# Half of the one-hot times low-gate products on ScalarE, token by token

## The chip, the cores and the metric

One core of a Trainium2 chip runs the whole program in one launch. The metric is the device time of one execution in microseconds (us); three runs of the kernel before are shown, and their median counts.

## The reference, cut to what matters

Two transformer blocks over 512 tokens of width 1024. The first mixes a pooling branch with a forgetting attention, the second mixes two attentions and ends in a PEER layer: eight heads each choose 16 of 16,384 experts for every token, with a gate each, and the experts' rows are summed.

```python
q = (xt @ w_q).reshape(TOKEN_BLOCK, PEER_HEADS, 2, PEER_HALF_DIM)
sc = jnp.einsum('thcd,chnd->thcn', q, sub_keys, preferred_element_type=jnp.float32)
top_s, top_i = lax.top_k(sc, k)
...
g = jax.nn.softmax(best_s, axis=-1)
pre = jnp.einsum('td,thkd->thk', xt, u[idx], preferred_element_type=jnp.float32)
coef = (g * jax.nn.gelu(pre, approximate=False)).astype(v.dtype)
return jnp.einsum('thk,thkd->td', coef, v[idx])
```

An expert's number is 128 I + J, with I and J between 0 and 127. Only how the gates g are spread over the experts is touched here.

## The kernel before, in words

The first 128 tokens gather their experts' rows by indirect DMA. The other 384 tokens (ND) take all 16,384 experts densely: for each of 128 groups of 128 experts, `u_stage` multiplies the group's u rows by the tokens (24 matmuls of 384 columns), a Gelu follows (`u_gelu`, L1445), the result is multiplied by a dense gate matrix and then by the v rows. Every fp32 operand is split in two fp32r halves: ScalarE writes `hi` (L1389), VectorE the rest `lo` (L1390), and three matmuls (L150 to L152) use them.

The dense gates are built first. `by_slot` (L1579 to L1588) transposes I, J and g of 128 tokens, so that the partition is the slot (head and choice) and the column the token. ScalarE casts I and J to fp16 (`I2`, `J2`) and writes the high half of 16384 g; VectorE subtracts for the low half (`g2[:, 0]`, `g2[:, 1]`). Each value stands twice in a row, for pairs of columns.

Then 24 groups of 16 tokens follow. `one_hots(b)` (L1649) makes on VectorE, over 16 x 128 columns: `aa`, where I equals the column (L1656); `oh`, where J does (L1657); and `bb`, `oh` times the high and times the low gates (L1659, twice). `aa` and `bb` have two buffers, `oh` has one. `products(b)` multiplies `aa` by `bb` with 32 small matmuls into four PSUM banks (L1670); ScalarE copies each bank out to `stage` (L1671) and issues the write of `stage` to DRAM (L1672). Before that, the same turn of the loop runs one group of dense u work ahead (`run_ahead`, L1440): `prep` for the group after the next matmuls (L1389 on ScalarE, L1390 on VectorE), `u_stage` on TensorE, Gelu on ScalarE. There are 21 such groups for 25 turns; the turns b = 0, 8, 16 and 24 have none.

```python
for b in range(n_b + 1):
    if NU - after - ua["n"] > left - min(left, left * (b + 1) // n_b):
        run_ahead(1, V)
    new = one_hots(b) if b < n_b else None
    if job:
        products(job)
    job = new
```

The schedule is manual here: each engine takes its instructions in the order in which the program issues them. In turn b that is, on ScalarE: `hi` of `prep`, Gelu, four copies of products(b-1), the DMA issue. On VectorE: `lo` of `prep`, `aa`, `oh`, `bb` twice. On TensorE: `u_stage`, products(b-1). SyncE loads one group of u rows for each `prep`; GpSimd has nothing to do in these turns.

Of the kernel before, what the change touches and what calls it, by code (L numbers as in the profile page):

```python
# [16 lines left out]
AF = mybir.ActivationFunctionType  # L17
OP = mybir.AluOpType
# [42 lines left out]
def hybrid_mla_peer_kernel(ctx: ExitStack, tc: tile.TileContext, x, meta, gains, rows, bforget, wf, w1v, w1u, poolw,  # L61
                           wup, wout, pos, w2v, w2u, wcq, wckv, wuq, wukv, wo, wpq, skT, uT, peer_u, peer_v, out, stop=None):
    nc = tc.nc
    V, S, G, PE = nc.vector, nc.scalar, nc.gpsimd, nc.tensor
# [10 lines left out]
    def bank(tag, bufs):  # L75
        return ps.tile([128, 512], F32, name=tag, tag=tag, bufs=bufs)

    def mm_bank():
        return bank("mm", 2)
# [97 lines left out]
    def tok(tt):  # L177
        return slice(tt * 128, (tt + 1) * 128)
# [69 lines left out]
    with ExitStack() as c1:  # L248
# [92 lines left out]
        b = mm_bank()  # L341
# [104 lines left out]
        for h in range(H):  # L446
            b = bank("s" if h % 2 else "pt", 2)
# [3 lines left out]
        b = bank("mi", 1)  # L451
# [175 lines left out]
        for uu in range(4):  # L627
# [6 lines left out]
            c = uu  # L634
            b = bank("s" if c % 2 else "pt", 2)
# [682 lines left out]
    ND = T - 128  # L1318
# [3 lines left out]
    def tP(shape, name, dt=F32, tag=None, bufs=None):  # L1322
        return pP.tile(shape, dt, name=name, tag=tag or name, bufs=bufs)
# [2 lines left out]
    I2 = tP([128, ND, 2], "I2", F16)  # L1326
    J2 = tP([128, ND, 2], "J2", F16)
    g2 = tP([128, 2, ND, 2], "g2", F16)
    gg0 = tP([128, 8, 16], "gg0")
    idx = tP([128, 128], "idx", I32)  # L1330
    pre = tP([128, 128], "pre")
# [210 lines left out]
    for h in range(8):  # L1542
# [13 lines left out]
        for m in range(2):  # L1556
            b = bank("s" if m else "pt", 2)
# [21 lines left out]
    def by_slot(tt):  # L1579
        b = bank("s" if tt % 2 else "pt", 2)  # L1580
        for n, src in enumerate((Ia, Ja, gg)):
            PE.transpose(b[:, tok(n)], src[:, tt].rearrange("p h k -> p (h k)"), ident)
        sl = slice((tt - 1) * 128, tt * 128)
        bc = lambda n: b[:, tok(n)].unsqueeze(2).to_broadcast([128, 128, 2])
        S.copy(I2[:, sl, :], bc(0))
        S.copy(J2[:, sl, :], bc(1))
        S.activation(g2[:, 0, sl, :], bc(2), AF.Copy, scale=16384.0)
        V.scalar_tensor_tensor(g2[:, 1, sl, :], bc(2), 16384.0, g2[:, 0, sl, :], op0=OP.mult, op1=OP.subtract)  # L1588

    for tt in range(1, TT):  # L1590
        by_slot(tt)
# [7 lines left out]
    NB, GJ = 16, 8  # L1599
# [49 lines left out]
    def one_hots(b):  # L1649
        t0 = b * NB  # L1650
        io = iota.rearrange("p (a s) -> p a s", s=2).unsqueeze(1).to_broadcast([128, NB, 64, 2])
        wide = lambda x: x[:, t0:t0 + NB, :].unsqueeze(2).to_broadcast([128, NB, 64, 2])
        aa = pG.tile([128, NB, 64, 2], F16, name="aa", tag="aa", bufs=2)
        oh = pG.tile([128, NB, 64, 2], F16, name="oh", tag="oh", bufs=1)
        bb = pG.tile([128, 2, NB, 64, 2], F16, name="bb", tag="bb", bufs=2)
        V.tensor_tensor(aa, wide(I2), io, op=OP.is_equal)  # L1656
        V.tensor_tensor(oh, wide(J2), io, op=OP.is_equal)  # L1657
        for c in range(2):
            V.tensor_tensor(bb[:, c], oh, wide(g2[:, c]), op=OP.mult)  # L1659
        return b, aa, bb  # L1660

    def products(job):
# [16 lines left out]
# [7 lines that stand above are left out]
# [80 lines left out]
    for n in range(2):  # L1766
        for tt in range(3):
            c = slice(n * 512, (n + 1) * 512)
# [79 lines left out]
```

## Time and profile before

| what | value |
|---|---|
| median of 3 runs | 1994.22 us (1994.12 to 1996.31) |
| the profiled execution | 1997.35 us |
| its span in the trace | 1995.2 us |
| mean granted TensorE clock | 0.988 of full |
| PE busy | 1943.4 us, 97% |
| DVE (VectorE) busy | 1370.7 us, 69% |
| ACT (ScalarE) busy | 768.6 us, 39% |
| chain that ended last | PE 92%, DVE 3%, ACT 2%, POOL 2% |

PE is TensorE's matmuls, PEld its weight loads, POOL GpSimd, SP SyncE. "Idle before" in a row is the time that an engine stood still just before an instruction, with what ended it. The chain that ended last is followed back from the last instruction to what released each step. Issuing a DMA isn't counted as busy. The loop of 24 groups lies between 972 and 1120 us.

### The profile page before, as it was taken

To read this page: it belongs to the slowest core of one execution; us is meant where nothing else is said; L and a number is where in the kernel's file an instruction comes from. 1 tells how busy PE (TensorE), PEld (TensorE's weight loads), DVE (VectorE), ACT (ScalarE), POOL (GpSimd) and SP (SyncE) were. 2 spreads that over 40 slices of the span, in tenths; PEclk is the share of its full clock that TensorE was granted. 3 is DMA by queue.
4 is the path that set the end of the run, shared out by engine and by line. 5 is a ranking of instruction groups with operands and counts; after the bars stand their busy time and mean duration, and the time that the engine had idled before them with its cause. 6 is when DMAs were issued, how large, how long until landed. Compare 5 with 4: busy or idle time off the path is not lost.

```text
span 1995.2 us, 27005 instructions
## 1 busy us (share of the span) xinstructions
PE 1943.4 (97%) x10297; PEld 1668.0 (84%) x10297; DVE 1370.7 (69%) x2571; ACT 768.6 (39%) x1228; POOL 590.9 (30%) x479
## 2 busy tenths in 40 slices
PE   7999999999997999999999999999999999999998
PEld 5777688777886778999899988888888888888887
DVE  4224422654476657999799678878787777777876
ACT  4223323245475442222455433333333333333332
POOL 1001100200048114665300034444443444344441
PEclk9999999999999999999999999999999999999999
DMA  4211122422111123312688889898898988888885
GB/s 151 99 64 43 43 85 85 134 89 76 40 67 43 48 92 139 106 61 76 189 253 254 285 307 332 308 334 295 309 330 315 322 317 321 321 317 317 306 309 190
DMA packets 138130, 387.63 MB, mean 194 GB/s; under 512 B 10625, under 2 KB 59905, under 8 KB 129809
## 3 DMA queue, kind: packets, MB, share of 16 engines
q1 hardware_dynamic: 48576, 216.65, 30.4%
q0 software_dynamic: 36864, 134.23, 19.6%
q10 hardware_dynamic: 52560, 35.03, 6.1%
q8 instruction: 80, 1.31, 0.3%
q14 instruction: 50, 0.40, 0.1%
HBM read 357.04 MB, written 28.84 MB: 193 GB/s over the span
## 4 chain that ended last, share of the span: by engine, by line
PE 92%; DVE 3%; POOL 2%; ACT 2%; issue 1%; DMA 1%; ACTq 0%; SPq 0%; DVEq 0%; POOLq 0%
PE mm L150 15%; PE mm L152 14%; PE mm L151 14%; PE s L151 4%; PE s L152 4%; PE pt L151 4%; PE pt L152 4%; PE s L150 4%; PE pt L150 4%; PE mi L150 2%; PE mi L152 2%; PE mi L151 2%; PE av L151 1%; PE av L152 1%; PE av L150 1%; PE av L1044 1%
## 5 line engine op out<-in xcount | busy, mean ns | idle before, releaser
L1617 POOL DMA_INDIRECT gat<-in_peer_u,idx x128 | 162.3, 1268 | 409.6 <-DVE pre L1631 373.8
L1617 POOL DMA_INDIRECT gat<-in_peer_v,idx x128 | 184.2, 1439 | 234.6 <-DVE acc L1635 211.6
L1389 ACT ACTIVATE vhi<-xt 128x1024 fp32r<-128x1024 f32 x97 | 103.0, 1062 | 247.1 <-issue 159.9
L1390 DVE TENSOR_TENSOR vlo<-xt,vhi 128x1024 fp32r<-128x1024 f32 x97 | 118.7, 1224 | 115.4 <-ACT vhi L1389 113.5
L150 PE MATMUL mm<-h_hi,uhi 128*128 128x384 f32 x568 | 193.0, 340 | 0.0
L152 PE MATMUL mm<-h_hi,ulo 128*128 128x384 f32 x568 | 191.3, 337 | 1.4 <-POOL ulo L1390 1.4
L151 PE MATMUL mm<-h_lo,uhi 128*128 128x384 f32 x568 | 191.1, 336 | 0.0
L130 DVE TENSOR_TENSOR wlo<-wraw,whi 128x2048 fp32r<-128x2048 f32 (+1 forms) x42 | 96.1, 2289 | 136.5 <-ACT whi L129 136.4
L1635 DVE SCALAR_TENSOR_TENSOR acc<-gat,pre,acc 128x1024 f32<-128x1024 f32 x128 | 164.1, 1282 | 2.2 <-DMA gat<-in_peer_v,idx 1.2
L1631 DVE CUSTOM_DVE_ANT_0 gat<-gat,xt 128x1024 f32<-128x1024 f32 x128 | 155.7, 1221 | 11.2 <-DMA gat<-in_peer_u,idx 11.2
L152 PE MATMUL mm<-h_hi,h_lo 128*128 128x384 f32 x456 | 153.7, 337 | 2.5 <-POOL h_lo L1390 2.5
L150 PE MATMUL mm<-h_hi 128*128 128x384 f32 x456 | 154.7, 339 | 0.0
L151 PE MATMUL mm<-h_lo,h_hi 128*128 128x384 f32 x456 | 153.4, 336 | 0.0
L129 ACT ACTIVATE whi<-wraw 128x2048 fp32r<-128x2048 f32 (+2 forms) x53 | 97.5, 1840 | 111.6 <-PE mm L151 59.0
L150 PEld LDWEIGHTS mm<-h_hi,uhi 128*128 128x128 f32 x568 | 107.5, 189 | 1.8
L152 PEld LDWEIGHTS mm<-h_hi,ulo 128*128 128x128 f32 x568 | 107.1, 189 | 2.1 <-POOL ulo L1390 2.1
L151 PEld LDWEIGHTS mm<-h_lo,uhi 128*128 128x128 f32 x568 | 107.3, 189 | 1.8
L150 PE MATMUL mm<-hT_hi,whi 128*128 128x512 f32 x256 | 104.7, 409 | 1.3 <-DVE fz L417 1.0
L151 PE MATMUL mm<-hT_lo,whi 128*128 128x512 f32 x256 | 102.1, 399 | 0.0
L152 PE MATMUL mm<-hT_hi,wlo 128*128 128x512 f32 x256 | 102.1, 399 | 0.0
L152 PE MATMUL pt<-vhi,w_lo 128*128 128x512 f32 x256 | 100.2, 392 | 0.0
L152 PE MATMUL s<-vhi,w_lo 128*128 128x512 f32 x256 | 100.2, 392 | 0.0
(586 smaller groups left out, 5060.5 us busy)
## 6 DMA issues: line engine op xcount, KB each, us to landing
xt<-in_peer_v SPq DMA_DIRECT2D x97, 512.0 KB
xt<-in_uT SPq DMA_DIRECT2D x95, 512.0 KB
Gd<-stage ACTq DMA_DIRECT2D x24, 1024.0 KB
gate<-Gd SPq DMA_DIRECT2D x16, 1536.0 KB
raw<-in_uT SPq DMA_DIRECT2D x33, 512.0 KB
wraw<-in_w1u SPq DMA_DIRECT2D x16, 1024.0 KB
raw<-in_peer_v SPq DMA_DIRECT2D x31, 512.0 KB
wraw<-in_wpq SPq DMA_DIRECT2D x8, 1024.0 KB
```

The source lines that it names most:

```text
L129: S.activation(hi[:, :n], r[:, :n], AF.Copy)
L130: lo_eng["e"].tensor_tensor(lo[:, :n], r[:, :n], hi[:, :n].bitcast(F32), op=OP.subtract)
L150: PE.matmul(o, L[0], R[0], start=start, stop=False)
L151: PE.matmul(o, L[0], R[1], start=False, stop=False)
L152: PE.matmul(o, L[1], R[0], start=False, stop=stop)
L1044: PE.matmul(av[:, col(h, qt):col(h, qt) + 64], pts[i][:, c + j * 128:c + (j + 1) * 128], src[:, j, h * 64:(h + 1) * 64], start=(j == 0), s ...
L1389: S.activation(hi, src, AF.Copy)
L1390: eng.tensor_tensor(lo, src, hi.bitcast(F32), op=OP.subtract)
L1617: G.indirect_dma_start(out=t, out_offset=None, in_=peer_u if kind == "u" else peer_v, in_offset=bass.IndirectOffsetOnAxis(ap=idx[:, s:s + ...
L1631: V.tensor_tensor_reduce(t, t, xt0, 1.0, 0.0, op0=OP.mult, op1=OP.add, accum_out=pre[:, s:s + 1])
L1635: V.scalar_tensor_tensor(acc, t, pre[:, s:s + 1], acc, op0=OP.mult, op1=OP.add)
```

## The change

The low half of `bb` is made by both engines: VectorE multiplies the first 8 tokens of a group, ScalarE the other 8, one token for each instruction (128 columns, Copy with a scale that is one fp32 value for each partition). For that scale, `by_slot` makes on ScalarE an fp32 copy `glo` of the low gates of these tokens, right behind VectorE's subtraction.

```diff
+    glo = tP([128, ND // 2], "glo")
...
         V.scalar_tensor_tensor(g2[:, 1, sl, :], bc(2), 16384.0, g2[:, 0, sl, :], op0=OP.mult, op1=OP.subtract)
+        S.copy(glo[:, (tt - 1) * 64:tt * 64].rearrange("p (b t) -> p b t", t=8),
+               g2[:, 1, sl, 0].rearrange("p (b t) -> p b t", t=16)[:, :, 8:16])
...
         V.tensor_tensor(oh, wide(J2), io, op=OP.is_equal)
-        for c in range(2):
-            V.tensor_tensor(bb[:, c], oh, wide(g2[:, c]), op=OP.mult)
+        V.tensor_tensor(bb[:, 0], oh, wide(g2[:, 0]), op=OP.mult)
+        V.tensor_tensor(bb[:, 1, 0:8], oh[:, 0:8], wide(g2[:, 1])[:, 0:8], op=OP.mult)
+        for t in range(8, NB):
+            S.activation(bb[:, 1, t].rearrange("p a s -> p (a s)"), oh[:, t].rearrange("p a s -> p (a s)"), AF.Copy,
+                         scale=glo[:, 8 * b + t - 8:8 * b + t - 7])
         return b, aa, bb
```

In program order the eight scalings of turn b stand on ScalarE between the Gelu of turn b and the four copies of products(b-1).

## Rows read from the trace of the kernel before

**Rows 1.** Page, first part: busy time of each engine (share) x instructions.
```profile
PE 1943.4 (97%) x10297; PEld 1668.0 (84%) x10297; DVE 1370.7 (69%) x2571; ACT 768.6 (39%) x1228; POOL 590.9 (30%) x479
```

**Rows 2.** Stretches: length, busy PE, PEld, DVE, ACT, POOL, granted clock, DMA share, GB/s.
```profile
976.00:978.00 2.00, 1.04 (x10) 0.95 (x11) 2.00 (x2) 0.00 (x0) 0.00 (x0) 0.57 0.89 324
...
1018.00:1020.00 2.00, 0.24 (x2) 0.11 (x2) 2.00 (x2) 0.76 (x2) 0.00 (x0) 1.00 0.64 244
...
1022.00:1024.00 2.00, 2.00 (x17) 2.00 (x15) 1.97 (x3) 1.46 (x3) 0.00 (x0) 0.50 0.72 205
1024.00:1026.00 2.00, 2.00 (x13) 2.00 (x12) 1.30 (x2) 1.11 (x2) 0.00 (x0) 0.99 0.48 139
...
1034.00:1040.00 6.00, 6.00 (x59) 5.84 (x57) 5.83 (x6) 3.58 (x6) 0.00 (x0) 1.00 0.91 259
```

**Rows 3.** The chain that ended last, in order of time: start us, us, what.
```profile
981.07 0.32 PE mm L151
...
1020.86 0.85 PE pt L1670 x8
...
1034.03 0.46 PE s L1670 x8
...
1040.05 0.46 PE s L1670 x8
```

**Rows 4.** ScalarE in order of time, one steady turn: start us, us, instruction [idle before].
```profile
1034.06 0.49 ACT L1445 ACTIVATE Gn<-mm 128x384 f32<-128x384 f32 x1 [2.00 <-PE mm L152]
1034.52 0.58 ACT L1671 COPY stage<-s 128x512 f32<-128x512 f32 x1
...
1036.61 0.37 ACTq L1672 DMA_DIRECT2D Gd<-stage  x1
1037.02 1.06 ACT L1389 ACTIVATE h_hi<-raw 128x1024 fp32r<-128x1024 f32 x1 [0.44 <-DVE bb L1659]
```

**Rows 5.** VectorE in order of time, the same turn.
```profile
1034.37 1.22 DVE L1657 TENSOR_TENSOR oh<-J,iota 128x2048 f16<-128x2048 f16 x1
1035.62 2.36 DVE L1659 TENSOR_TENSOR bb<-oh,g 128x2048 f16<-128x2048 f16 x2
1038.12 1.23 DVE L1390 TENSOR_TENSOR h_lo<-raw,h_hi 128x1024 fp32r<-128x1024 f32 x1
1039.26 1.22 DVE L1656 TENSOR_TENSOR aa<-I,iota 128x2048 f16<-128x2048 f16 x1
1040.40 1.22 DVE L1657 TENSOR_TENSOR oh<-J,iota 128x2048 f16<-128x2048 f16 x1
```

**Rows 6.** VectorE in order of time, turn 8, which has no run-ahead.
```profile
1017.86 2.36 DVE L1659 TENSOR_TENSOR bb<-oh,g 128x2048 f16<-128x2048 f16 x2
1020.13 1.22 DVE L1656 TENSOR_TENSOR aa<-I,iota 128x2048 f16<-128x2048 f16 x1
```

**Rows 7.** Line L1657, all 24: duration min/median/max ns, first and last start us.
```profile
L1657 DVE TENSOR_TENSOR oh<-J,iota x24: 1216/1219/1221, 973.5 to 1112.5; 128x2048 f16<-128x2048 f16 x24
```

**Rows 8.** Groups of instructions between 972 and 1120 us: the Gelus of run-ahead.
```profile
L1445 ACT ACTIVATE Gn<-mm 128x384 f32<-128x384 f32 x11 | 5.4, 490 | 22.8 <-PE mm L152 22.8
...
L1445 ACT ACTIVATE Gq<-mm 128x384 f32<-128x384 f32 x10 | 4.9, 490 | 20.0 <-PE mm L152 20.0
```

**Rows 9.** ScalarE at 128 columns elsewhere: L1158 with a pointer, L588 without (mean ns).
```profile
645.51 0.38 ACT L1158 ACTIVATE sbf<-s,nm 128x128 f32<-128x128 f32 x1
645.77 0.21 ACT L1158 ACTIVATION_READ_ACCUMULATOR sbf<-s,nm 128x1 f32 x1
...
L588 ACT COPY pts<-pt 128x128 f32<-128x128 f32 x4 | 1.0, 262 | 5.0 <-PE pt L586 5.0
```

**Rows 10.** All engines in order of time, by_slot and the first one-hot.
```profile
970.13 0.41 ACT L1585 CAST I<-pt 128x256 f16<-128x256 f32 x1
...
970.30 0.42 DVE L1588 SCALAR_TENSOR_TENSOR g<-s,g 128x256 f16<-128x256 f32 x1 [5.64 <-ACT g L1587]
...
972.37 1.22 DVE L1656 TENSOR_TENSOR aa<-I,iota 128x2048 f16<-128x2048 f16 x1
```

## The prediction, made blind

> **What bounds the kernel now.** I read the page's busy times first: TensorE is busy for 97% of the span, VectorE for 69%, ScalarE for 39% [rows 1]. Such averages say little about 150 us out of 1995, so I cut out the loop that the change touches. In the stretches a steady turn of 6 us has TensorE busy throughout at full clock, VectorE for 5.83 us and ScalarE for 3.58 us [rows 2]. The reader is to see two things there: TensorE sets the pace, and VectorE is only a little behind it. The chain of waits agrees: the products of one turn start at 1034.03 us, those of the next at 1040.05, so a turn lasts 6.02 us [rows 3], and nothing but TensorE stands between. Only around the turns without run-ahead does TensorE wait for VectorE's `bb`: between 1018 and 1020 us it is busy for 0.24 of 2 us [rows 2]. So work taken from VectorE can pay only at these few stalls; in the other turns TensorE needs its 6.02 us anyway.
>
> Then I read the order of time on the two engines that the change joins. ScalarE in one turn: Gelu at 1034.06, first copy at 1034.52, DMA issue at 1036.61, `hi` for a later group at 1037.02 [rows 4]. The 2.00 us before the Gelu are all the slack it has. VectorE: `lo` starts at 1038.12, as soon as `hi` is written, then `aa` at 1039.26, `oh` at 1040.40 [rows 4, 5]. Today this dependence runs one way only within a turn: VectorE waits for ScalarE's `hi`, and ScalarE never waits for a one-hot of the same turn.
>
> **The change part by part.**
>
> *The removed half of a multiply.* A pair of full multiplies takes 2.36 us [rows 5], so one is 1.18 and half of one about 0.59; VectorE gains 0.59 us a turn. In steady turns it lies beside TensorE's work and is worth nothing.
>
> *The eight scalings.* The nearest row is an ACTIVATE of 128 columns with a pointer operand (there the bias): it lasts 0.38 us, and the next instruction starts 0.26 us after it [rows 9]. I take 0.26, that is 2.08 us for eight. No row has eight of them in succession from fp16. The upper bound is no overlap at all, 0.37 us each (2.96), nearly that row's own duration. The lower bound is the copy without a pointer, 0.262 us, less the 0.11 to 0.12 that instructions overlap: 0.15 each (1.20). I take 0.26 because that row has the same width and a pointer.
>
> [...]
>
> *The order.* The scalings of turn b read `oh` of turn b and stand on ScalarE ahead of the copies of products(b-1), the DMA issue, and `hi` of turn b+1. `lo` of b+1 waits for that `hi`, and on VectorE `aa` and `oh` of b+1 stand behind `lo`. The scalings of b+1 need that `oh`. This closes a ring, once a turn, through two engines that each keep their order:
>
> - start of `oh` to its first reader: 1034.37 to 1035.62, 1.25 us [rows 5];
> - eight scalings: 2.08;
> - first copy to `hi`, with the DMA issue in it: 1034.52 to 1037.02, 2.50 [rows 4];
> - `hi` to `lo`: 1037.02 to 1038.12, 1.10 [rows 4, 5];
> - `lo` to `aa` 1.14, `aa` to `oh` 1.14 [rows 5].
>
> The sum is 9.21 us a turn, against 6.02 now. The Gelu (0.46) fits in while ScalarE waits for `oh`. VectorE's two multiplies (1.18 and 0.59 us behind `oh`) end long before the next `lo`, and the single `oh` buffer is free again 3.33 us after its start, so neither adds. TensorE's 6.02 us of work fit in 9.21 with a turn to spare: products(b-1) have their operands a whole turn before the copies want them.
>
> *How often.* 21 groups run ahead in the loop [rows 8], so 21 turns contain the ring. The first (0 to 1) has no copies in it: 1.25 + 2.08 + 1.10 + 1.14 + 1.14 = 6.71 us. The others are 20 x 9.21 = 184.2. The turns 8 and 16 have no `hi` and `lo`; there ScalarE sets the pace with scalings and copies, 2.08 + 2.50 = 4.58 us each, 9.2 together (VectorE's way to the next `oh`, where `aa` follows the multiplies at once [rows 6], is 1.25 + 1.18 + 0.59 + 1.14 = 4.16, shorter). From the first `oh` to the last that makes 6.7 + 184.2 + 9.2 = 200.1 us; now it is 1112.5 - 973.5 = 139.0 [rows 7]. The change is +61.1 us.
>
> *The copies to `glo`.* ScalarE now waits in `by_slot` for VectorE's subtraction, which ends at 970.30 + 0.42 = 970.72; with about 0.2 for wake-up and a copy of 64 columns the next cast starts at about 970.93 rather than 970.13 [rows 10]. Queued behind it are the casts of the next 128 tokens. Two of the three waits lie ahead of the first `aa`: 2 x 0.8 = 1.6 us later, with TensorE already waiting there (busy 1.04 us of 2 just after [rows 2]). Bounds: 0 if it were hidden, 2.4 with the third.
>
> *The end of the loop and the queues.* Behind the last `oh` come scalings, copies and products in about the time that the last multiply and products take now; I put 0 there. SyncE's loads of u rows and the writes of `stage` follow the slower turns, with the DMA share at 0.91 in the steady turn now [rows 2], so they only get easier. What comes after the loop shifts as a whole, since TensorE is what it waits for.
>
> **Sum:** 61.1 + 1.6 = +62.7 us. The profiled execution, 1997.35 us (2.15 around its span of 1995.2), would become 2060.1; it is 3.1 us above the median of 1994.22, so for the median I predict 2057 us. With 23 turns that hold scalings inside the path, the bounds of a scaling move this by 23 x 8 x 0.11 = 20 us either way: 2037 to 2077.
>
> **The rivals.**
>
> [...]
>
> *No ring.* If ScalarE could take `hi` of the next turn ahead of the scalings, the ring would be open. ScalarE would then have 0.46 + 2.08 + 2.50 + 1.06 = 6.10 us in a turn of 6.02, so 21 x 0.08 = 1.7 us slower; with 1.6 from `by_slot`, less 0.59 at each of four stalls where TensorE waits for `bb` (2.4), the time would be 1995 us: no change. It decides if the order on ScalarE isn't the program's. Against it, the order in the trace is exactly the program's [rows 4].
>
> **How the numbers follow.** The ring has 0.78, TensorE at half clock 0.09, no ring 0.07; 0.06 is left for something between no ring and the lower bound. The ring with its bounds is 2037 to 2077, and up to 2095 takes in the half clock: together a little over 8 in 10 once the ring itself can miss its bounds. About 0.2% (4 us) is what a measurement of this kernel can tell from no change. Faster needs the open ring with scalings at their lower bound: 0.02; within 0.2%: 0.06; slower: 0.92.
>
> **What would show it.** Right: the starts of `oh` 9.2 us apart in steady turns, 4.6 at turns 8 and 16, the last `oh` some 200 us after the first; ScalarE idle before its first scaling until VectorE's `oh`, VectorE idle before `lo` until `hi`; each scaling 0.26 us after the one before; TensorE idle or at half clock in each turn. [...]

## The result, and the profile after

The changed kernel takes 2065.02 us (median of 5 runs, 2063.69 to 2066.7) against 1994.22 before: a ratio of 1.0353, 95% interval 1.0342 to 1.0364. It is slower by 70.8 us; 2057 was forecast, with 2037 to 2077 as the range of the ring and up to 2095 with the half clock. The profiled execution took 2065.02 us with a span of 2063.3, 68.1 us longer than the span of before.

The page's first part:

```profile
PE 1959.2 (95%) x10297; PEld 1675.9 (81%) x10297; DVE 1359.0 (66%) x2571; ACT 822.2 (40%) x1423; POOL 590.9 (29%) x479
```

Beside [rows 1], VectorE has 11.7 us less to do and ScalarE 53.6 more, and all engines have a smaller share but ScalarE. No engine became the bound; what grew is waiting. Line by line, `oh` marks the turns of the loop (duration min/median/max ns, first and last start us):

```profile
L1660 DVE TENSOR_TENSOR oh<-J,iota x24: 1216/1218/1221, 975.3 to 1180.4; 128x2048 f16<-128x2048 f16 x24
```

First to last it is 205.1 us, 139.0 before [rows 7]: 66.1 of the 68.1 us. The first `oh` starts 1.8 us later, and from the last one to the end it is 882.9 us, 882.7 before. So nothing outside the loop and `by_slot` changed.

One steady turn on ScalarE (start us, us, instruction, idle before):

```profile
1054.43 2.45 ACT L1664 ACTIVATE bb<-oh,glo 128x128 f16<-128x128 f16 x8 [2.05 <-DVE oh L1660]
1056.78 0.56 ACT L1677 COPY stage<-s 128x512 f32<-128x512 f32 x1
...
1058.81 0.37 ACTq L1678 DMA_DIRECT2D Gd<-stage  x1
1059.23 1.06 ACT L1390 ACTIVATE uhi<-xt 128x1024 fp32r<-128x1024 f32 x1 [0.44 <-ACT stage L1677]
```

and on VectorE:

```profile
1053.18 1.22 DVE L1660 TENSOR_TENSOR oh<-J,iota 128x2048 f16<-128x2048 f16 x1
...
1060.32 1.22 DVE L1391 TENSOR_TENSOR ulo<-xt,uhi 128x1024 fp32r<-128x1024 f32 x1 [4.06 <-ACT uhi L1390]
1061.46 1.22 DVE L1659 TENSOR_TENSOR aa<-I,iota 128x2048 f16<-128x2048 f16 x1
```

Read them as one circle. ScalarE idles until `oh`, scales, copies, issues, makes `hi`; VectorE idles 4.06 us for that `hi`, makes `lo`, `aa`, `oh`; and ScalarE's next scalings wait for that `oh`. Each engine waits for the other once a turn. The starts of `oh` lie 9.42 us apart in steady turns, and the steps around the circle are 1.25 + 2.35 + 2.45 + 1.09 + 1.14 + 1.14 = 9.42 us. Before, the same two engines stood at [rows 4, 5] with VectorE hardly idle in such a turn (5.83 of 6 us busy [rows 2]).

Who waited for whom, in the loop (us in total, times, longest us):

```profile
ACT bb L1664 <- DVE oh L1660: 67.9, 22, 3.2
DVE ulo L1391 <- ACT uhi L1390: 43.0, 11, 4.7
DVE h_lo L1391 <- ACT h_hi L1390: 41.4, 10, 4.8
...
PE s L1676 <- ACT stage L1677: 21.5, 14, 7.4
```

TensorE's clock, in stretches of the loop (columns as in [rows 2]):

```profile
1000.00:1010.00 10.00, 8.41 (x58) 7.77 (x59) 5.90 (x7) 5.79 (x14) 0.00 (x0) 0.83 0.60 176
...
1040.00:1050.00 10.00, 6.85 (x47) 6.95 (x48) 6.08 (x7) 8.92 (x25) 0.00 (x0) 0.57 0.52 153
...
1080.00:1090.00 10.00, 6.91 (x57) 6.20 (x58) 5.91 (x7) 5.79 (x14) 0.00 (x0) 1.00 0.62 176
...
1110.00:1120.00 10.00, 6.09 (x49) 6.19 (x50) 6.84 (x7) 8.61 (x24) 0.00 (x0) 0.66 0.60 175
```

In most steady turns TensorE is busy for 7 of 10 us and still has a granted clock of 1.00. In stretches of 2 us the clock falls to 0.50 at both ends of the loop, around turns 8 and 16 (1040 and 1110 us), and in three of the steady turns (near 1002, 1101 and 1162 us); those three are 9.42 us long like the others. At turn 8 TensorE does no work for 7.4 us:

```profile
1043.15 1.01 PE L1676 MATMUL s<-bb,aa 128*128 128x128 f16 x8 [7.37 <-DVE aa L1659]
```

The trace puts the end of this wait down to an `aa` that ends at the same moment. In the program these products, those of group 7, read the `aa` of the turn before; what they lack until 1043.10 us is the bank that the first copy behind the scalings frees (1042.54 and 0.56 us, shown further below).

### The profile page after: what moved, and what is told of

It is laid out like the page before. It is cut to its first block, busy times and chain, and to the rows that moved or that the text cites. A ratio compares the mean times of both kernels' runs of the same rounds, so it can differ in the third digit from the quotient of the medians.

```text
span 2063.3 us, 27190 instructions
## 1 busy us (share of the span) xinstructions
PE 1959.2 (95%) x10297; PEld 1675.9 (81%) x10297; DVE 1359.0 (66%) x2571; ACT 822.2 (40%) x1423; POOL 590.9 (29%) x479
## 3 DMA queue, kind: packets, MB, share of 16 engines
q0 software_dynamic: 36864, 134.23, 18.8%
## 4 chain that ended last, share of the span: by engine, by line
PE 83%; ACT 7%; DVE 6%; POOL 2%; issue 1%; DMA 1%; ACTq 0%; SPq 0%; DVEq 0%; POOLq 0%
PE mm L150 13%; PE mm L152 13%; PE mm L151 13%; PE s L151 4%; PE s L152 4%; PE pt L152 4%; PE pt L151 4%; PE s L150 4%; PE pt L150 4%; ACT bb L1664 3%; ACT stage L1677 2%; PE mi L150 2%; PE mi L152 2%; PE mi L151 2%; PE av L151 1%; PE av L152 1%
```

## The experiments

The theory is the ring. Its rivals: TensorE at half clock, ScalarE's total work, the scalings' own price wherever they stand, and no influence of the order.

**Four tokens on ScalarE (four_tokens).**

```diff
-        V.tensor_tensor(bb[:, 1, 0:8], oh[:, 0:8], wide(g2[:, 1])[:, 0:8], op=OP.mult)
-        for t in range(8, NB):
+        V.tensor_tensor(bb[:, 1, 0:12], oh[:, 0:12], wide(g2[:, 1])[:, 0:12], op=OP.mult)
+        for t in range(12, NB):
```

> Only 4 tokens of each group on ScalarE, 12 on VectorE. Ring (scalings, copies, DMA issue, hi, lo, aa, oh, back to the scalings): each scaling left out takes 0.295 us from every turn that holds them, 4 x 0.295 x 23 = 27 us, so about 2038 us and 8.2 us between the oh of steady turns. TensorE at half clock as the pace: turns stay at 9.4 us or more, about 2065 us. ScalarE's total work as the pace: with 5.2 us a turn it falls below TensorE's 6.0, about 1996 us.

Measured: 2039.85 us, 25.2 less than the changed kernel (expected: 27). The loop:

```profile
L1660 DVE TENSOR_TENSOR oh<-J,iota x24: 1216/1218/1220, 976.0 to 1155.9; 128x2048 f16<-128x2048 f16 x24
```

179.9 us instead of 205.1. Steady turns are 8.26 us long (expected: 8.2), 0.29 us less for each scaling left out, so the scalings lie on the path, and neither TensorE's clock nor ScalarE's total sets the pace. The rest of the expected 27 is missing at turns 8 and 16: there `oh` follows `oh` after 4.40 us, which is VectorE's own work.

**Scalings behind the copies (copies_first).** `scalings(job)` is the loop over t taken out of `one_hots`; nothing else changes.

```diff
         if job:
             products(job)
+        if new:
+            scalings(new)
         job = new
```

> The eight scalings of a turn issued behind the four copies and the DMA issue instead of ahead of them. Ring: the copies (2.45 us from the first to hi) leave it, what is left is 1.25 + 2.35 + 1.10 + 1.14 + 1.14 = 7.0 us a turn, still over TensorE's 6.0: 20 x 1.0 us over before and 1.5 from by_slot, about 2014 us. ScalarE's total work as the pace (6.4 us a turn, unchanged): about 2003 us. No influence of the order at all: 2065 us.

Measured: 2018.77 us. Two `oh` in succession:

```profile
1038.22 1.22 DVE L1660 TENSOR_TENSOR oh<-J,iota 128x2048 f16<-128x2048 f16 x1
...
1045.17 1.22 DVE L1660 TENSOR_TENSOR oh<-J,iota 128x2048 f16<-128x2048 f16 x1
```

The turn is 6.95 us (expected: 7.0). With exactly the same instructions, order alone is worth 46 us: the copies left the ring, the rest of it still binds. The loop is 159.0 us long, 20.0 more than before, which is the 20 x 1.0 of the expectation, though not turn by turn: 4.1 of it lie at turns 8 and 16. The total is 21.4 us above the profiled execution of before; the 5 us over the expected 2014 are mostly the 3.1 by which that execution stands above its median.

**Scalings behind the next `hi` (late8).** They are issued in the next turn, between `prep` and the Gelu.

```diff
-    def run_ahead(n, eng):
+    def run_ahead(n, eng, between=None):
...
                 prep("u", ahead_of[i + 1], eng)
+            if between:
+                between()
...
-            run_ahead(1, V)
+            run_ahead(1, V, (lambda: scalings(job)) if job else None)
+        elif job:
+            scalings(job)
         new = one_hots(b) if b < n_b else None
```

> The eight scalings of a turn issued in the next turn, behind its hi and ahead of its Gelu; all instructions are kept. Ring: hi no longer stands behind the scalings of the turn before, the ring is open; ScalarE then has 0.46 + 2.36 + 2.45 + 1.06 = 6.3 to 6.4 us a turn against TensorE's 6.0, so 21 x 0.35 = 7 us over before, less what the shorter VectorE gives back at turns 8, 16 and 24: 1992 to 2004 us. If the scalings themselves (their price, or reading beside VectorE) are what costs, not their place: 2040 us or more.

Measured: 1997.21 us, 1.0014 of before (1.0005 to 1.0024). ScalarE in order of time:

```profile
1035.80 0.47 ACT L1446 ACTIVATE Gn<-mm 128x384 f32<-128x384 f32 x1
...
1038.62 1.06 ACT L1390 ACTIVATE h_hi<-raw 128x1024 fp32r<-128x1024 f32 x1 [0.44 <-ACT stage L1682]
1039.59 2.43 ACT L1670 ACTIVATE bb<-oh,glo 128x128 f16<-128x128 f16 x8
1041.93 0.47 ACT L1446 ACTIVATE Gn<-mm 128x384 f32<-128x384 f32 x1
```

The Gelu has no idle time before it and comes every 6.13 us: ScalarE is full and sets the pace, a little over TensorE's 6.02. All 192 scalings and `glo` are still there, and 68 of the 71 us are gone. That settles place against price. The loop is no longer than before (138.6 us against 139.0), since its start and the turns around 8 and 16 make good what the 6.13 us cost; the first `oh` starts 2.4 us later.

**`lo` on GpSimd (after_pool_lo).** The scalings stay where the change put them; VectorE is taken out of the wait for `hi` instead.

```diff
-            run_ahead(1, V)
+            run_ahead(1, G)
         new = one_hots(b) if b < n_b else None
```

> The changed kernel with lo of the run-ahead on GpSimd within the loop, so that VectorE no longer waits for hi. Ring: open as well; ScalarE's 6.4 us a turn set the pace, about 2003 us, if GpSimd's lo (2.4 to 2.9 us in the trace of before) stays under a turn. If GpSimd is slowed beside VectorE to over 6 us a lo, TensorE waits for lo: over 2010 us. Order without influence: 2065 us.

Measured: 2004.61 us. The ring, opened at its other side, goes as well: most turns are 6.2 to 6.8 us long. GpSimd's `lo` takes 2.47 us on average in the loop (21 of them), but VectorE's `aa` takes up to 3.09 us there instead of 1.22 (below). Which engine sets the pace of these turns was not worked out.

**The pointer's price (no_pointer).** The low gates of the 8 tokens are left out.

```diff
-                         scale=glo[:, 8 * b + t - 8:8 * b + t - 7])
+                         scale=1.0)
```

> The changed kernel with the constant scale 1.0 in place of the pointer to glo; the low gates of the 8 tokens are left out. It prices the operand. If the pointer costs what the two rows of 128 columns in the trace of before differ by (0.36 to 0.38 against 0.26 us), eight scalings take 8 x 0.1 = 0.8 us less, and the ring hands this on in 23 turns: 18 us, about 2047 us. If the distance of 0.295 us between scalings is something else (fp16, a wait between neighbours): within 3 us of 2065.

Measured: 2046.23 us, 18.8 less. One turn without the pointer:

```profile
1055.01 1.71 ACT L1664 ACTIVATE bb<-oh 128x128 f16<-128x128 f16 x8 [3.18 <-DVE oh L1660]
1056.62 0.56 ACT L1677 COPY stage<-s 128x512 f32<-128x512 f32 x1
```

Eight take 1.61 us from the first to the copy, 2.35 with the pointer: 0.20 against 0.29 us each. The median duration falls from 386 to 294 ns. The loop is 16.5 us shorter, near 23 x 0.74 = 17; most of the rest is a first `oh` that starts 1.5 us earlier.

**The copies to `glo` alone (glo_only).** All sixteen tokens stay on VectorE.

```diff
-        V.tensor_tensor(bb[:, 1, 0:8], oh[:, 0:8], wide(g2[:, 1])[:, 0:8], op=OP.mult)
-        for t in range(8, NB):
-            S.activation(bb[:, 1, t].rearrange("p a s -> p (a s)"), oh[:, t].rearrange("p a s -> p (a s)"), AF.Copy,
-                         scale=glo[:, 8 * b + t - 8:8 * b + t - 7])
+        V.tensor_tensor(bb[:, 1], oh, wide(g2[:, 1]), op=OP.mult)
```

> The copies to glo alone: all sixteen tokens stay on VectorE and nothing reads glo. In the trace the first aa comes 1.5 us behind the Gelu-and-cast chain of before (two waits of 0.5 us for the subtraction and two copies of 0.16 to 0.2 us), the turns of the loop stay at 6.02 us with stalls at 8, 16 and 24: 1995 to 1998 us, hardly to be told from before. Were glo a part of the ring's 66 us, 2000 us or more.

Measured: 1994.93 us, not to be told from before. `glo` has no part in the 66 us of the loop.

**Looking for a gain: four tokens late (late4).** late8 with the first edit, 12 tokens on VectorE.

> As late8, with 4 tokens of each group on ScalarE and 12 on VectorE. The ring is open and ScalarE's 5.2 us a turn lie under TensorE's 6.02, so steady turns fall from 6.13 to 6.02 us: some 2 us less than late8's 1997, 1994 to 1996, no better than before, since VectorE still reaches the turns 8, 16 and 24 too late. If ScalarE's load isn't what made late8's turns 6.13, no difference to late8.

Measured: 1991.83 us, 0.9983 of before (0.9974 to 0.9993): faster, where I had expected no gain. Steady turns are 6.02 us long, so ScalarE's load was what made late8's 6.13. In the profiled execution, at 1997.25 us the longest of the ten, the first `oh` starts 6.7 us later than before, and the loop is 133.6 us long, 5.4 less than before.

**One-hots ahead of the run-ahead, in the kernel before (before_hots_first).**

```diff
+        new = one_hots(b) if b < n_b else None
         if NU - after - ua["n"] > left - min(left, left * (b + 1) // n_b):
             run_ahead(1, V)
-        new = one_hots(b) if b < n_b else None
```

> The kernel before, with one change of order: in each turn the one-hots are issued ahead of the run-ahead, so that VectorE makes aa, oh, bb of a turn before its lo. If the stalls at turns 8, 16 and 24 come from lo standing (and waiting for hi) ahead of the one-hots, they go: about 2 us of idle and 1.9 us at half clock at each, 3 x 3.9 = 12 us, so 1982 to 1986 us. If VectorE's 5.9 us of a 6.02 us turn leave lo too late for the next u_stage, or VectorE's total work sets the stalls: 1992 us or more.

Measured: 1998.73 us, 1.0027 of before (1.0013 to 1.0041). The gain did not come; the second of the two expectations did. TensorE's waits around the loop:

```profile
PE mm L152 <- DVE ulo L1390: 4.6, 2, 2.4
PE mm L152 <- DVE h_lo L1390: 3.1, 2, 2.4
```

The products of turns 8 and 16 no longer wait, but the next `u_stage` waits up to 2.4 us for its `lo` instead. A turn without run-ahead takes TensorE 1.8 us and VectorE 4.7, and a steady turn gives VectorE only 0.2 us back (5.83 of 6 us busy [rows 2]). So, as I read it, VectorE's work over the two turns makes the stall, and the order only chooses who stands in it.

**The same with four tokens on ScalarE (four_hots_first).** The order of before_hots_first, the scalings between `hi` and the Gelu of their own turn, one copy to `glo`.

> The change without its ring: 4 tokens on ScalarE, one-hots ahead of the run-ahead on VectorE, scalings behind hi and ahead of the Gelu of the same turn, one copy to glo behind the three by_slot. Stalls at turns 8, 16 and 24 go as in before_hots_first, and VectorE has 0.3 us of slack more: 1980 to 1986 us. If the scalings on ScalarE are worth something, it is faster than before_hots_first; if VectorE is off the path there too, both are the same within 2 us.

Measured: 1994.25 us, 1.0002 of before (0.9992 to 1.0011). No change, a miss too, though faster than before_hots_first by 4.5 us.

**One copy to `glo` (late4_glo, late6_glo).** late4, and the same with 6 tokens on ScalarE, with:

```diff
-        S.copy(glo[:, (tt - 1) * 64:tt * 64].rearrange("p (b t) -> p b t", t=8),
-               g2[:, 1, sl, 0].rearrange("p (b t) -> p b t", t=16)[:, :, 8:16])
...
         by_slot(tt)
+    S.copy(glo.rearrange("p (b t) -> p b t", t=8), g2[:, 1, :, 0].rearrange("p (b t) -> p b t", t=16)[:, :, 8:16])
```

> late4 with one copy to glo behind the three by_slot instead of one in each. It takes the 1.5 us of by_slot off the path and leaves the loop as in late4 (133.6 us from the first oh to the last, against 139.0 before): 1990 to 1991 us, faster than before by 0.2 to 0.3%. If late4's gain was chance, within 0.1% of before.

> As late4_glo with 6 tokens on ScalarE: 0.46 + 6 x 0.295 + 2.45 + 1.06 = 5.7 us a turn, still under TensorE's 6.02. VectorE has 0.15 us less in each turn, so each of the three stalls gets some 0.3 us shorter: 1989 to 1991 us, 0 to 1 us under late4_glo. If ScalarE already binds at 5.7 us, slower than late4_glo by up to 3 us.

Measured: 1987.73 us, 0.9973 of before (0.9962 to 0.9984), and 1988.95, 0.9975 (0.9965 to 0.9984). Both beat both kernels; the two can't be told apart. The first is 2.3 us below its expected range. Turn 8 on TensorE, first before, then in late4_glo:

```profile
1019.14 0.23 PE L1670 MATMUL s<-bb,aa 128*128 128x128 f16 x1 [1.13 <-DVE bb L1659]
1020.27 0.59 PE L1670 MATMUL s<-bb,aa 128*128 128x128 f16 x7 [0.90 <-DVE bb L1659]
```

```profile
1016.24 0.23 PE L1680 MATMUL s<-bb,aa 128*128 128x128 f16 x1 [1.08 <-DVE bb L1662]
1017.11 0.55 PE L1680 MATMUL s<-bb,aa 128*128 128x128 f16 x7 [0.64 <-DVE bb L1663]
```

and the stretches around it in late4_glo:

```profile
1016.00:1018.00 2.00, 1.12 (x17) 1.00 (x18) 2.00 (x3) 1.58 (x5) 0.00 (x0) 1.00 0.81 263
1018.00:1020.00 2.00, 2.00 (x25) 2.00 (x23) 1.97 (x3) 1.75 (x4) 0.00 (x0) 1.00 1.02 290
```

The stall is 0.3 us shorter, and the granted clock stays at 1.00 where it fell to 0.50 before [rows 2]. Of the 5.5 us by which the loop shrank (133.5 us), 1.9 lie around turn 8, as many around turn 16, and 1.7 in the first three turns, where the clock falls in both kernels but is back sooner in late4_glo (0.83 from 970 to 980 us, 1.00 from 980 to 990; before, 0.50 between 978 and 982 and 0.73 between 982 and 984). The shorter idle time alone gives 0.3 of each 1.9; that the rest goes with the clock is read from the stretches, and no run changed the clock alone.

In late4, late4_glo and late6_glo the clock stays at 1.00 at turns 8, 16 and 24. The shorter stall is not shown to be the reason: in glo_only TensorE idles at turn 8 for the same 1.13 and 0.90 us as before, and the clock stays up there all the same (1.00 from 1010 to 1020 us too), while it falls at turn 16 (0.87 from 1060 to 1070 us):

```profile
1020.00:1022.00 2.00, 2.00 (x34) 2.00 (x33) 2.00 (x2) 1.55 (x4) 0.00 (x0) 1.00 1.02 290
1022.00:1024.00 2.00, 2.00 (x13) 2.00 (x13) 1.97 (x3) 1.56 (x3) 0.00 (x0) 1.00 0.74 214
...
1060.00:1070.00 10.00, 7.69 (x80) 7.24 (x79) 9.52 (x10) 5.27 (x10) 0.00 (x0) 0.87 0.89 255
```

What decides it stays open.

## Why the prediction was right

*The ring.* Right in place and in kind: the waits stand where they were foretold, and five runs agree that shortening it (four_tokens, no_pointer), taking steps out of it (copies_first) or opening it (late8, after_pool_lo) moves the time by what the steps say. late8 gives back all but 3 of the 71 us, after_pool_lo all but 10.

*Its length.* 9.42 us for 9.21. The step that was mis-sized is the eight scalings: 2.35 us for 2.08. I had taken the 0.26 us from a row with a pointer [rows 9], where the next instruction reads an accumulator. Between two scalings it is 0.294 us in the changed kernel and 0.20 us without the pointer (no_pointer), so the pointer costs 0.09 us here; what makes the distance in the row shorter, no run shows. In 23 turns the 0.27 us are 6.2 us more, and the way from the first copy to `hi` (2.45 for 2.50) gives 1 us back: the 5.0 us by which 205.1 exceeds 200.1.

*The turns 8 and 16.* ScalarE sets the pace there, as foretold, with 4.79 us (4.58):

```profile
1040.19 2.44 ACT L1664 ACTIVATE bb<-oh,glo 128x128 f16<-128x128 f16 x8 [3.19 <-DVE oh L1660]
1042.54 0.56 ACT L1677 COPY stage<-s 128x512 f32<-128x512 f32 x1
...
1044.98 2.46 ACT L1664 ACTIVATE bb<-oh,glo 128x128 f16<-128x128 f16 x8 [0.45 <-ACT stage L1677]
```

The sign that I named, starts of `oh` 4.6 us apart, was wrong: VectorE makes the `oh` of turn 8 after 4.13 us without waiting for ScalarE, and the next one 10.1 us later.

*`by_slot`.* 1.6 us were forecast. ScalarE waits for the subtraction as described:

```profile
970.20 0.42 ACT L1588 ACTIVATE g<-s 128x256 f16<-128x256 f32 x1
...
970.65 0.42 DVE L1589 SCALAR_TENSOR_TENSOR g<-s,g 128x256 f16<-128x256 f32 x1 [5.66 <-ACT g L1588]
971.11 0.24 ACT L1590 CAST glo<-g 128x64 f32<-128x64 f16 x1 [0.49 <-DVE g L1589]
971.26 0.36 ACT L1586 CAST I<-pt 128x256 f16<-128x256 f32 x1
```

The next cast comes 1.06 us behind the Activate that the subtraction waited for (970.20), where it took 0.27 between neighbours before; twice the difference is 1.6. From the end of the subtraction (971.07) to that cast it is 0.19 us, about 0.2 in the forecast. Of the 1.8 us by which the first `oh` is late, 0.35 were there already ahead of `by_slot`, which leaves some 1.5 for it.

*TensorE.* The 2095 us at the top of the range, TensorE at half clock as the pace, are a term that no run shows. In its place the runs showed turns of 9.42 us, both at a granted clock of 1.00 and in the three steady turns where it falls to 0.50; there the ring hid the lower clock. TensorE idle or at half clock in each turn was one of my signs: in the steady turns it idles, busy for some 7 of 10 us, and the lower clock came in those three only. I also wrote that products have a turn to spare; they wait 21.5 us for banks that the copies free late. Neither costs anything while the ring is longer.

*The sum.* 62.7 us were forecast, 67.7 us separate the two profiled executions, and the difference is the 5 us of the ring. The medians are 70.8 apart because the profiled execution of before stood 3.1 us above its median. I had taken these 3.1 us off for the forecast, and the changed kernel's profiled execution is its median, so 2057 is 8 us too low: 5 by the ring and 3 by that step.

## What to carry to other kernels

Before work moves to an idle engine, write down both engines' orders and look for a circle: an engine at 39% has no room if the moved work stands, in its queue, between something it must deliver and something that depends on the result. The sum around the circle is then the length of a turn, whatever the shares say, wherever it is longer than the busiest engine's own work (here 9.42 us against TensorE's 6.02). The same work placed behind the delivery costs 3 us instead of 71 (late8), and half of it there gains 0.3% (late4_glo); half of it in the old place still costs some 45 us (four_tokens).

## What had not been expected of the hardware

In after_pool_lo VectorE's `aa` took up to 3.09 us beside a `lo` of GpSimd, and 1.22 us without one. GpSimd's `lo`, twice:

```profile
1032.57 2.35 POOL L1391 TENSOR_TENSOR h_lo<-xt,h_hi 128x1024 fp32r<-128x1024 f32 x1 [8.73 <-ACT h_hi L1390]
...
1047.00 2.36 POOL L1391 TENSOR_TENSOR h_lo<-raw,h_hi 128x1024 fp32r<-128x1024 f32 x1 [5.77 <-ACT h_hi L1390]
```

VectorE's `aa` beside the first, one with no GpSimd work beside it, and one beside the second:

```profile
1032.91 3.09 DVE L1659 TENSOR_TENSOR aa<-I,iota 128x2048 f16<-128x2048 f16 x1 [0.71 <-PE pt L1676]
...
1042.48 1.22 DVE L1659 TENSOR_TENSOR aa<-I,iota 128x2048 f16<-128x2048 f16 x1 [3.48 <-PE pt L1676]
...
1048.51 1.93 DVE L1659 TENSOR_TENSOR aa<-I,iota 128x2048 f16<-128x2048 f16 x1 [1.80 <-PE pt L1676]
```

The first ends at 1036.00, 1.08 us after GpSimd ended at 1034.92, as if it had begun only then; the last one, of 1.93 us, ends at 1050.44, 1.08 us after GpSimd's 1049.36 too. What holds VectorE up there, no run shows.
